# A recurrent mixer by seven products: order of loads, low parts a pair ahead, a later scaling of each head's output

## The chip, the cores and the metric

The kernel runs on one core of a Trainium2 chip. The metric is device time in microseconds of one execution; lower is better. The engines are TensorE (PE, with its weight loads PEld), VectorE (DVE), ScalarE (ACT), GpSimd (POOL) and SyncE (SP). Each works through its own queue in order; they meet by semaphores. DMA transfers are issued from the queues of SP and POOL here.

## The reference

One step of a two-layer decoder trunk on 512 prompt tokens and 8 x 4 new tokens, 544 columns in all, width 1024, all in f32. Layer 0 is a Mamba-2 mixer and a squared-ReLU MLP, layer 1 an HGRN2 mixer and another MLP, each behind an RMS norm and added to the residual. The change is in the HGRN2 mixer:

```python
proj = (u @ w_in).astype(jnp.float32)            # 1024 -> 4096: q, f, v, g
q = silu(proj[..., :F]); fz = proj[..., F:2*F]; v = proj[..., 2*F:3*F]; g = proj[..., 3*F:]
logf = logaddexp(log_sigmoid(fz), log(max(lb, 1e-20)) + log_sigmoid(-fz))
k = (1.0 - lb) * sigmoid(-fz)
o, s = hgrn_chunk_scan(q, k, v, logf, state)     # S_t = diag(f_t) S_{t-1} + k_t v_t^T ; o_t = S_t^T q_t
o = group_rmsnorm(o, norm_w, 8) * silu(g)        # 8 heads of 128
return o @ w_out, s
```

The states of the prompt and of the 8 sequences are outputs too.

## The kernel before, in words

Activations lie transposed: eight tiles `x[k]` of 128 features x 544 columns. f32 products are made of three products of a rounded format: both operands are split into a rounded high part and a rest, and high x high, high x low and low x high are added in PSUM. A unit of weights is a piece of 128 x 1024 (512 KB). There are three ways to a low part. `split` rounds the piece on ACT (`hi`) and subtracts on DVE (`lo = raw - hi`), in halves of 512 columns. Units in `by_load` have ACT write the negated rounded piece and a DMA from POOL add the weight to it in memory (L251, L252). Units loaded already rounded (kind "c", a DMA of POOL that converts, L205) do the same as one piece in `low_ahead` (L286, tile `lo`, one buffer).

The mixer's input has 32 units, four for each of 8 heads (q, f, v, g). The first four (head 0) are plain products (`product`, `project`). The other 28 are 14 pairs: two units with both halves of the rows and columns make a 2 x 2 block product that is done with seven products ("forms") instead of eight, in the order of `SLOTS`: p1, p2, n6, q7, n5, p3, q4, each 12 matmuls of 128 x 272, and pairs overlap: p1, p2 of pair i, then p3 of i-1, n6, q7 of i, q4 of i-1, n5 of i. p1 and p2 use the rounded piece ("c") and its `lo`; the other five use sums of pieces: `v` holds two halves of 512 columns, to which POOL DMAs add a third half (kind "va", L212); "a22" is a half by itself (L208); `s2 = v + a22` on DVE (tile `s`, L303), to which another POOL DMA adds later (L311). Each of the five is then split on ACT and DVE (`fh_*`, `fl_*`).

The list `loads` gives the order of loads and `jobs` that of conversions. A conversion calls loads up to three places past its own (`at + 3`), and `ahead` runs conversions until four halves wait for use. Instructions written out are then put in each engine's order by a planner that has its own costs and issues what is ready by them, so an instruction can run well ahead of its place in the text. Tiles of one tag share `bufs` buffers; a new one waits for the last use of the old. `mx` tiles are four PSUM banks (tag "mx"); `acc` tiles are two pairs of banks.

Between the matmuls, `tick()` runs background generators, two ticks per form. `operands` (norm, sums of halves) and `split_sums` prepare the right-hand sides. For each head `levels` computes the attention inside 128-token chunks by doubling (tiles `pa`, `K`, `q`, `T`), started by `complete` when f is there, with a wait in ticks, and `states` the rest: masks the values for eight sequences (`vm`), chunk states (`pS`, `S`), output (`po`, `pzs`), mean square (`oms`), its power -1/2 on POOL (`or`, L1626), scaling into `o2` (in the profile `o`, L1627 and L1630), then new states by two matmuls `pn` with four DVE updates `hst` each (L1637), and transposing back (`pt`). Last comes the output projection (`pho`), 8 units in two halves of heads. DVE's `f`, `g` and so on (L1441 to L1445) collect the seven products from PSUM and set its banks free.

Of the kernel before, what the change touches and what calls it, by code (L numbers as in the profile page):

```python
# [112 lines left out]
def trunk(ctx: ExitStack, tc: tile.TileContext, io):  # L113
# [58 lines left out]


    by_load = {ub + i for ub in (U_MLP, U_MLP2) for i in (1, 2, 3, 4, 5, 6, 8, 9)}
    by_load |= set(range(U_HGRN_IN, U_HGRN_IN + 4)) | set(range(U_HGRN_OUT, U_MLP2))
    plans = [plan_mlp(U_MLP, False)]
    hgrn_pairs, hgrn_forms = _hgrn_plan(U_HGRN_IN)
    pair_at = {u: i for i, u in enumerate(hgrn_pairs)}
    loads += [("u", U_HGRN_IN + i) for i in range(3)] + [("c", hgrn_pairs[0]), ("u", U_HGRN_IN + 3)]
    at = {x: len(loads) + i for i, x in enumerate(loads[-5:], -5)}  # L180
    for u in range(U_HGRN_IN, U_HGRN_IN + 4):
        jobs.append((("u", u), at["u", u]))
    for i, u in enumerate(hgrn_pairs):
        loads += [(kind, v) for kind, j in (("v", i), ("c", i + 1), ("va", i), ("a22", i)) for v in hgrn_pairs[j : j + 1]]
        at |= {x: len(loads) + i for i, x in enumerate(loads[-4:], -4)}
    for name, u in hgrn_forms:
        jobs.append(((name, u), at[{"p1": "c", "p2": "c", "q4": "a22", "n6": "a22"}.get(name, "va"), u]))
    for u in range(U_HGRN_OUT, U_MLP2):
        loads.append(("u", u))
        jobs.append((("u", u), len(loads) - 1))  # L190
# [95 lines left out]
    def low_ahead(u):  # L286

        hi = loaded["c", u]
        lo = mp["w"].tile([P, 1024], F32R, tag="lo12", bufs=1, name=f"lo{u}")
        nc.scalar.activation(lo, hi.bitcast(F32), AF.Copy, scale=-1.0)  # L290
        nc.gpsimd.dma_start(lo, io["W"][u], accum_op=ADD)
        lows[u] = lo

    def pair_form(name, u):

        i = pair_at[u]
        if name in ("p1", "p2"):
            c = slice(0, 512) if name == "p1" else slice(512, 1024)
            return [loaded["c", u][:, c]], [lows[u][:, c]]
        v = loaded["v", u]  # L300
        if name == "n6":
            s2 = mp["w"].tile([P, 512], F32, tag="s2", bufs=1, name=f"s2_{u}")
            nc.vector.tensor_tensor(s2, v[:, 512:], loaded["a22", u], ADD)  # L303
            loaded["s2", u] = s2
        raw = {"n6": ("s2", 0), "q7": ("v", 512), "n5": ("v", 0), "p3": ("s2", 0), "q4": ("a22", 0)}[name]
        raw = loaded[raw[0], u][:, raw[1] : raw[1] + 512]
        hi = wcv.tile([P, 512], F32R, tag="whi", name=f"fh{u}_{name}")
        lo = wcv.tile([P, 512], F32R, tag="wlo", name=f"fl{u}_{name}")
        split(raw, hi, lo)
        if name == "q7":  # L310
            nc.gpsimd.dma_start(loaded["s2", u], io["W"][u][:, 512:], accum_op=ADD)  # L311
        if name == "n5" and i + 1 < len(hgrn_pairs):
            low_ahead(hgrn_pairs[i + 1])
        return [hi], [lo]

    def form(name, u):
# [947 lines left out]
    def hgrn(then):  # L1264
# [91 lines left out]
        def product(u):  # L1356
            w = unit(u)
            ps = acc_tile(f"ps{u}")
            products(ps, w, uops, True, True, run=8, every=3)
            state["live"] -= 2  # L1360
            return ps

# [20 lines left out]
        def complete(u):  # L1383

            h, j = divmod(u - u0, 4)
            hc = slice(h, h + 1)
            d = heads[h]
            if j == 0:
                gate(d["q"], f"sq{h}")
            if j == 1:  # L1390
                f = d["f"]
                K = d["K"] = pool.tile([P, 640], F32, tag="K", bufs=2, name=f"K{h}")
                nf = K[:, :T]
                nc.scalar.activation(nf, f, AF.Sigmoid, scale=-1.0)
                nc.scalar.activation(f, f, AF.Sigmoid)
                nc.vector.scalar_tensor_tensor(f, nf, lbf[:, hc], f, MUL, ADD)
                nc.vector.tensor_tensor(d["QQ"][:, 1], d["q"], f, MUL)
                nc.scalar.activation(nf, nf, AF.Copy, scale=olb[:, hc])
                background(levels(h, d["QQ"], K, f, d), f"hl{h}", wait=2.5)
            if j == 2:  # L1400
                d["vz"] = d["v"]
            if j == 3:
                gate(d["g"], f"sg{h}")
# [8 lines left out]
        def seventh(name, u):  # L1412
# [6 lines left out]
                d["b"] = mx(f"hb{u}")[:, :HF]  # L1419
            ps = d[{"p2": "b", "q7": "c", "q4": "c"}.get(name, "a")]  # L1420
            hi, lo = take((name, u))
            n = 0
            for k in range(4):
                oh, ol = fops[name, k]
# [7 lines left out]
                        tick()  # L1432
            if name not in ("p1", "p2"):
                state["live"] -= 1
            keep = {"p1": "s1", "n6": "sv", "n5": "sw"}.get(name)
            with tc.high_priority():
                if keep:
                    d[keep] = pool.tile([P, HF], F32, tag=keep, bufs=1 + (keep == "sv"), name=f"{keep}_{u}")
                    nc.scalar.copy(d[keep], ps)
                if name == "p2":  # L1440
                    nc.vector.tensor_tensor(target(u)[:, :HF], ps, d["s1"], ADD)  # L1441
# [125 lines left out]
        def states(h, d):  # L1567
# [7 lines left out]
            for c in range(4):  # L1575
# [4 lines left out]
            o2 = pool.tile([P, 5, P], F32, tag="o2", name=f"o2{h}")  # L1580
            qm = o2[:, :2].rearrange("p a (b c) -> p (a b) c", c=NS)
            nc.vector.tensor_tensor(qm, Q[:, sc].unsqueeze(1).to_broadcast([P, SEQS, NS]), seqcol, MUL)
            vm = pool.tile([P, SEQS, P], F32R, tag="vm", name=f"vm{h}")
            nc.vector.tensor_tensor(
                vm, vq.unsqueeze(1).to_broadcast([P, SEQS, P]), seqrow.unsqueeze(2).to_broadcast([P, SEQS, P]), MUL
            )
            yield pace
            pS = mx(f"pS{h}")
            for c in range(4):
# [34 lines left out]
            nc.vector.tensor_scalar(ms, ms, 1.0 / P, EPS, MUL, ADD)  # L1624
            r = pool.tile([P, 5], F32, tag="or", bufs=2, name=f"or{h}")
            nc.gpsimd.tensor_tensor(r, ms, half, ALU.pow)  # L1626
            nc.vector.tensor_tensor(  # L1627
                o2[:, :4], po.rearrange("p (a b) -> p a b", b=P), r[:, :4].unsqueeze(2).to_broadcast([P, 4, P]), MUL
            )
            nc.vector.tensor_scalar(o2[:NS, 4], pzs[:NS, :P], r[:NS, 4:5], None, MUL)  # L1630
            yield pace
            for i in range(2):
                pn = mx(f"pn{h}_{i}")
                nc.tensor.matmul(pn, kq, vm[:, 4 * i : 4 * i + 4].rearrange("p s v -> p (s v)"), start=True, stop=True)
                for j in range(4):
                    s = 4 * i + j
                    nc.vector.scalar_tensor_tensor(st[:, s], st[:, s], Ts[:, s : s + 1], pn[:, j * P : (j + 1) * P], MUL, ADD)  # L1637
                yield pace
            nc.sync.dma_start(io["hgrn_s"][h], st)
            yield pace  # L1640
# [237 lines left out]
```

## Time and profile before

| | |
|---|---|
| median of 3 runs | 1531.43 us (1529.78 to 1533.83) |
| profiled execution | 1532.86 us, its span 1531.1 us |
| granted TensorE clock, mean over the span | 0.987 |
| busy: PE, DVE, ACT, POOL | 97%, 83%, 62%, 19% |
| second mixer | about 814 to 1156 us |
| its transfers | 59.35 MB, 173 GB/s |

In the profile a row of waits reads: engine, line, "<-" what it waited for, microseconds in total, how often, the longest. A row of a timeline: start, length, engine, line, operation, tiles written <- read, and in brackets the idle time before it and what ended it. A row of one line's instructions has durations in ns (least/median/most). Tile names are without numbers; several tiles can have one name (`hb` and `hp` are accumulators of the seven products, `ps` those of the plain ones).

### The profile page before, as it was taken

Reading aid. Unit: us, or ns where it says so; the run is one execution under the profiler, and the core shown is the slowest. Engines: PE = TensorE matmul, PEld = TensorE weight load, DVE = VectorE, ACT = ScalarE, POOL = GpSimd, SP = SyncE. Lnnn points to the kernel's source line nnn. Section 1 sums busy time; section 2 is a strip of 40 time slices with the busy share of each in tenths; the row PEclk is TensorE's granted clock in tenths of the full one; section 3 lists DMA queues with packets and bytes.
Section 4 is the critical chain, followed back from the end, with each engine's and each line's share of the span. In section 5 each row is a group of like instructions: output and inputs, shape, how many; then the busy total and the mean of one; then the engine's idle time right before and its main releaser. Section 6 shows DMA issues by size and latency. Waiting matters only on the chain. (4 is left out here: it accounts for less than half of the span.)

```text
span 1531.1 us, 33266 instructions
## 1 busy us (share of the span) xinstructions
PE 1482.8 (97%) x12956; PEld 1414.5 (92%) x12956; DVE 1276.8 (83%) x2486; ACT 946.9 (62%) x1928; POOL 290.1 (19%) x392
## 2 busy tenths in 40 slices
PE   8999899999999999999998899999999999999996
PEld 7898889898999999999997788888898999999996
DVE  7978899879777879898898778888856989888895
ACT  5685756757447657585776445455555758576673
POOL 3122012120012111111103123332222111111101
PEclk9999999999999999999999999999999999999998
DMA  6376557483557565675749477878568567575741
GB/s 193 94 198 169 163 129 207 128 223 105 153 154 153 128 179 145 173 179 139 191 113 234 102 180 174 188 179 206 128 157 202 125 172 179 138 186 137 184 115 66
DMA packets 106862, 243.77 MB, mean 159 GB/s; under 512 B 18064, under 2 KB 22064, under 8 KB 106704
## 3 DMA queue, kind: packets, MB, share of 16 engines
q1 hardware_dynamic: 66560, 158.17, 31.3%
q0 software_dynamic: 38880, 82.33, 30.5%
q8 instruction: 102, 1.67, 0.4%
q10 hardware_dynamic: 1264, 1.14, 0.2%
q14 instruction: 56, 0.46, 0.1%
HBM read 224.41 MB, written 17.18 MB: 158 GB/s over the span
## 5 line engine op out<-in xcount | busy, mean ns | idle before, releaser
L220 POOL DMA_DIRECT2D v<-in_W x94 | 82.2, 1018 | 468.1 <-DVE fl_p L232 130.9
L405 PE MATMUL ps<-uh_s,whi 128*128 128x272 f32 x576 | 124.4, 297 | 4.2 <-DVE BC L603 2.4
L405 PE MATMUL ps<-ul_s,whi 128*128 128x272 f32 x576 | 120.1, 289 | 0.0
L231 ACT CAST whi<-raw 128x512 fp32r<-128x512 f32 x114 | 70.0, 616 | 79.1 <-PE ps L405 40.6
L405 PEld LDWEIGHTS ps<-uh_s,whi 128*128 128x128 f32 x576 | 90.2, 188 | 11.8 <-issue 8.5
L256 ACT CAST whi<-raw 128x512 fp32r<-128x512 f32 x90 | 55.3, 617 | 70.2 <-PE ps L405 20.9
L232 DVE TENSOR_TENSOR wlo<-raw,whi 128x512 fp32r<-128x512 f32 x114 | 80.0, 704 | 22.1 <-ACT whi L231 20.5
L405 PEld LDWEIGHTS ps<-ul_s,whi 128*128 128x128 f32 x576 | 90.4, 188 | 0.6 <-issue 0.3
L232 DVE TENSOR_TENSOR fl_p<-raw,fh_p 128x512 fp32r<-128x512 f32 x94 | 64.1, 689 | 28.9 <-ACT fh_p L231 24.5
L405 PE MATMUL ps<-uh_s,wlo 128*128 128x272 f32 x576 | 85.2, 288 | 0.0
L231 ACT CAST fh_p<-raw 128x512 fp32r<-128x512 f32 x94 | 57.6, 619 | 37.8 <-PE pp L1176 20.8
L252 POOL DMA_DIRECT2D wlo<-in_W x56 | 49.1, 941 | 164.8 <-ACT wlo L251 153.6
L405 PEld LDWEIGHTS ps<-uh_s,wlo 128*128 128x128 f32 x576 | 77.3, 188 | 1.0 <-issue 0.8
L596 DVE SCALAR_TENSOR_TENSOR cacc<-pre,vh,cacc 128x568 f32<-128x568 f32 x72 | 57.8, 802 | 5.8 <-ACT cacc L594 5.3
L231 ACT CAST fh_n<-v 128x512 fp32r<-128x512 f32 x61 | 37.8, 619 | 37.2 <-PE pp L1176 32.9
L231 ACT CAST fh_p<-s 128x512 fp32r<-128x512 f32 x61 | 37.8, 620 | 34.8 <-PE pc_q L1176 27.3
L284 POOL DMA_DIRECT2D wlo<-in_W x34 | 30.1, 1044 | 146.9 <-ACT wlo L281 133.6
L405 PE MATMUL po<-yh,whi 128*128 128x272 f32 x256 | 55.7, 298 | 1.2 <-ACT yh L231 1.2
L232 DVE TENSOR_TENSOR fl_n<-s,fh_n 128x512 fp32r<-128x512 f32 x61 | 42.1, 690 | 16.0 <-ACT fh_n L231 11.7
L1176 PE MATMUL pp<-m_tl,fh_n 128*128 128x272 f32 x192 | 55.3, 288 | 0.0
L1176 PE MATMUL pc_q<-m_th,fh_q 128*128 128x272 f32 x192 | 55.3, 288 | 0.0
L1176 PE MATMUL pc_q<-m_th,fl_q 128*128 128x272 f32 x192 | 55.3, 288 | 0.0
(549 smaller groups left out, 5836.0 us busy)
## 6 DMA issues: line engine op xcount, KB each, us to landing
raw<-in_W SPq DMA_DIRECT2D x147, 512.0 KB, 4.5
v<-in_W SPq DMA_DIRECT2D x122, 256.0 KB, 4.5
v<-in_W POOLq DMA_DIRECT2D x122, 256.0 KB, 5.6
wlo<-in_W POOLq DMA_DIRECT2D x90, 256.0 KB, 6.1
a<-in_W SPq DMA_DIRECT2D x61, 256.0 KB, 4.6
w<-cum_d POOLq DMA_DIRECT2D x16, 512.0 KB, 7.7
st<-in_ssm_in SPq DMA_DIRECT2D x16, 512.0 KB, 4.6
out_ssm_s<-st SPq DMA_DIRECT2D x16, 512.0 KB, 6.1
```

Of the source, the lines that this page charges most:

```text
L220: nc.gpsimd.dma_start(raw[:, c : c + 512], io["W"][u + 1][:, :512], accum_op=ADD)
L231: nc.scalar.copy(hi, raw)
L232: (eng or nc.vector).tensor_tensor(lo, raw, hi.bitcast(F32), SUB)
L252: nc.gpsimd.dma_start(lo[a], io["W"][u][:, 512 * a : 512 * a + 512], accum_op=ADD)
L256: nc.scalar.copy(hi[a], c)
L284: nc.gpsimd.dma_start(lows[u][a], io["W"][u][:, 512 * a : 512 * a + 512], accum_op=ADD)
L405: nc.tensor.matmul(ps[:, h, :HF], block(a, c0 + k * step), o[:, h * HF : (h + 1) * HF], start=(first and i == 0), stop=(last and i == len( ...
L596: nc.vector.scalar_tensor_tensor(acc, pre[:, i : i + 568], vh[:, wc + 24 * i : wc + 24 * i + 1], acc, MUL, ADD)
L1176: nc.tensor.matmul(ps, block(w, k * P), o, start=(name_ in ("p1", "p2", "q7") and k == 0 and j == 0), stop=(k == 3 and j == 2), skip_group ...
```

## The change

- Of the mixer's four plain units only the third and fourth make their low part by load; the first two are split on DVE, and their products go piece by piece (high, low of each k) instead of all high parts first (`run`). Of the eight output units the last four are split too.
- The order of loads: all four plain units, then the first rounded piece; for each pair "a22" comes before "va", and the list for pair 0 is written apart. n6 now takes its place in the list from "va" instead of from "a22".
- `lo` has two buffers; the next pair's is asked for behind the matmuls of p1, instead of with the conversion of n5. `s1` and `sw` share one buffer.
- The wait ahead of `levels` is 4.5 ticks instead of 2.5.
- `vm` is made in two halves of four sequences. The mean square's scale and offset go to POOL. `o` is scaled behind the first four state updates, followed by the second half of `vm`.

```diff
-    by_load |= set(range(U_HGRN_IN, U_HGRN_IN + 4)) | set(range(U_HGRN_OUT, U_MLP2))
+    by_load |= {U_HGRN_IN + 2, U_HGRN_IN + 3} | set(range(U_HGRN_OUT, U_HGRN_OUT + 4))
...
-    loads += [("u", U_HGRN_IN + i) for i in range(3)] + [("c", hgrn_pairs[0]), ("u", U_HGRN_IN + 3)]
-    at = {x: len(loads) + i for i, x in enumerate(loads[-5:], -5)}
+    loads += [("u", U_HGRN_IN + i) for i in range(4)] + [("c", hgrn_pairs[0])]
+    loads += [(kind, hgrn_pairs[j]) for kind, j in (("v", 0), ("c", 1), ("a22", 0), ("va", 0))]
+    at = {x: len(loads) + i for i, x in enumerate(loads[-9:], -9)}
...
-    for i, u in enumerate(hgrn_pairs):
-        loads += [(kind, v) for kind, j in (("v", i), ("c", i + 1), ("va", i), ("a22", i)) for v in hgrn_pairs[j : j + 1]]
+    for i in range(1, len(hgrn_pairs)):
+        loads += [(kind, v) for kind, j in (("v", i), ("c", i + 1), ("a22", i), ("va", i)) for v in hgrn_pairs[j : j + 1]]
...
-        jobs.append(((name, u), at[{"p1": "c", "p2": "c", "q4": "a22", "n6": "a22"}.get(name, "va"), u]))
+        jobs.append(((name, u), at[{"p1": "c", "p2": "c", "q4": "a22"}.get(name, "va"), u]))
...
-        lo = mp["w"].tile([P, 1024], F32R, tag="lo12", bufs=1, name=f"lo{u}")
+        lo = mp["w"].tile([P, 1024], F32R, tag="lo12", bufs=2, name=f"lo{u}")
...
-        if name == "n5" and i + 1 < len(hgrn_pairs):
-            low_ahead(hgrn_pairs[i + 1])
...
-            products(ps, w, uops, True, True, run=8, every=3)
+            products(ps, w, uops, True, True, run=8 if u in by_load else 0, every=3)
...
-                background(levels(h, d["QQ"], K, f, d), f"hl{h}", wait=2.5)
+                background(levels(h, d["QQ"], K, f, d), f"hl{h}", wait=4.5)
...
+            if name == "p1" and u != hgrn_pairs[-1]:
+                low_ahead(hgrn_pairs[pair_at[u] + 1])
...
-                    d[keep] = pool.tile([P, HF], F32, tag=keep, bufs=1 + (keep == "sv"), name=f"{keep}_{u}")
+                    d[keep] = pool.tile([P, HF], F32, tag="sv" if keep == "sv" else "sw", bufs=1 + (keep == "sv"), name=f"{keep}_{u}")
...
-            vm = pool.tile([P, SEQS, P], F32R, tag="vm", name=f"vm{h}")
...
+            def values_of(i):
+                vm = pool.tile([P, 4, P], F32R, tag="vm", name=f"vm{h}_{i}")
...
+            vm = values_of(0)
...
-            nc.vector.tensor_scalar(ms, ms, 1.0 / P, EPS, MUL, ADD)
+            nc.gpsimd.tensor_scalar(ms, ms, 1.0 / P, EPS, MUL, ADD)
...
-            nc.vector.tensor_tensor(
-                o2[:, :4], po.rearrange("p (a b) -> p a b", b=P), r[:, :4].unsqueeze(2).to_broadcast([P, 4, P]), MUL
-            )
-            nc.vector.tensor_scalar(o2[:NS, 4], pzs[:NS, :P], r[:NS, 4:5], None, MUL)
             yield pace
             for i in range(2):
...
+                if i == 0:
+                    nc.vector.tensor_tensor(
+                        o2[:, :4], po.rearrange("p (a b) -> p a b", b=P), r[:, :4].unsqueeze(2).to_broadcast([P, 4, P]), MUL
+                    )
+                    nc.vector.tensor_scalar(o2[:NS, 4], pzs[:NS, :P], r[:NS, 4:5], None, MUL)
+                    vm = values_of(1)
                 yield pace
```

More of the change, by code (lines that the diff above doesn't have):

```diff
@@ L294, in pair_form @@
     def pair_form(name, u):
-        i = pair_at[u]
         if name in ("p1", "p2"):
-            c = slice(0, 512) if name == "p1" else slice(512, 1024)
-            return [loaded["c", u][:, c]], [lows[u][:, c]]
+            return None, None
         v = loaded["v", u]
@@ L1421, in seventh @@
             hi, lo = take((name, u))
+            if name in ("p1", "p2"):
+                c = slice(0, 512) if name == "p1" else slice(512, 1024)
+                hi, lo = [loaded["c", u][:, c]], [lows[u][:, c]]
             n = 0
@@ L1582, in states @@
             nc.vector.tensor_tensor(qm, Q[:, sc].unsqueeze(1).to_broadcast([P, SEQS, NS]), seqcol, MUL)
-            vm = pool.tile([P, SEQS, P], F32R, tag="vm", name=f"vm{h}")
-            nc.vector.tensor_tensor(
-                vm, vq.unsqueeze(1).to_broadcast([P, SEQS, P]), seqrow.unsqueeze(2).to_broadcast([P, SEQS, P]), MUL
-            )
+            def values_of(i):
+                vm = pool.tile([P, 4, P], F32R, tag="vm", name=f"vm{h}_{i}")
+                nc.vector.tensor_tensor(
+                    vm, vq.unsqueeze(1).to_broadcast([P, 4, P]),
+                    seqrow[:, 4 * i : 4 * i + 4].unsqueeze(2).to_broadcast([P, 4, P]), MUL,
+                )
+                return vm
+            vm = values_of(0)
             yield pace
@@ L1623, in states @@
             nc.scalar.activation(o2[:NS, 4], pzs[:NS, :P], AF.Square, accum_out=ms[:NS, 4:5])
-            nc.vector.tensor_scalar(ms, ms, 1.0 / P, EPS, MUL, ADD)
+            nc.gpsimd.tensor_scalar(ms, ms, 1.0 / P, EPS, MUL, ADD)
             r = pool.tile([P, 5], F32, tag="or", bufs=2, name=f"or{h}")
             nc.gpsimd.tensor_tensor(r, ms, half, ALU.pow)
-            nc.vector.tensor_tensor(
-                o2[:, :4], po.rearrange("p (a b) -> p a b", b=P), r[:, :4].unsqueeze(2).to_broadcast([P, 4, P]), MUL
-            )
-            nc.vector.tensor_scalar(o2[:NS, 4], pzs[:NS, :P], r[:NS, 4:5], None, MUL)
             yield pace
@@ L1633, in states @@
                 pn = mx(f"pn{h}_{i}")
-                nc.tensor.matmul(pn, kq, vm[:, 4 * i : 4 * i + 4].rearrange("p s v -> p (s v)"), start=True, stop=True)
+                nc.tensor.matmul(pn, kq, vm.rearrange("p s v -> p (s v)"), start=True, stop=True)
                 for j in range(4):
@@ L1637, in states @@
                     nc.vector.scalar_tensor_tensor(st[:, s], st[:, s], Ts[:, s : s + 1], pn[:, j * P : (j + 1) * P], MUL, ADD)
+                if i == 0:
+                    nc.vector.tensor_tensor(
+                        o2[:, :4], po.rearrange("p (a b) -> p a b", b=P), r[:, :4].unsqueeze(2).to_broadcast([P, 4, P]), MUL
+                    )
+                    nc.vector.tensor_scalar(o2[:NS, 4], pzs[:NS, :P], r[:NS, 4:5], None, MUL)
+                    vm = values_of(1)
                 yield pace
```

## The prediction

> **What bounds the kernel now.** I read the page first, then the stretches of the changed stage, what TensorE (PE) waited for in it, the chain that ended last, and the engines' queues in order of time.
>
> ```profile
> span 1531.1 us, 33266 instructions
> PE 1482.8 (97%) x12956; PEld 1414.5 (92%) x12956; DVE 1276.8 (83%) x2486; ACT 946.9 (62%) x1928; POOL 290.1 (19%) x392
> ```
>
> PE is busy nearly all of the span, so only time in which PE stands still, or runs at a low clock, can be won. The second mixer lasts from 814 to 1156 us. Its stretches (PE, PEld, DVE, ACT, POOL busy; granted clock; DMA share; GB/s):
>
> ```profile
> 813.00:850.00 37.00, 31.51 (x325) 29.56 (x324) 32.27 (x79) 21.24 (x40) 13.31 (x20) 0.95 0.86 206
> 850.00:892.00 42.00, 33.33 (x302) 30.09 (x301) 28.84 (x70) 21.08 (x51) 10.11 (x13) 0.88 0.61 124
> ...
> 992.00:1026.00 34.00, 33.27 (x419) 30.11 (x420) 28.97 (x77) 18.54 (x47) 11.56 (x15) 1.00 0.80 190
> ```
>
> The first 79 us hold the loss: 14.2 us without PE and a lowered clock. A head in the steady part loses 0.7 us of 34. PE's waits in the whole stage:
>
> ```profile
> PE hp L1426 <- DMA lo<-in_W: 4.2, 1, 4.2
> PE ps L405 <- DVE q L1407: 3.9, 1, 3.9
> PE hp L1426 <- DVE f L1445: 2.9, 1, 2.9
> PE pn L1634 <- DVE o L1627: 2.7, 4, 1.2
> PE hp L1426 <- DVE hn_tl L232: 1.5, 2, 0.8
> PE ps L405 <- DMA wlo<-in_W: 1.4, 1, 1.4
> PE pa L1487 <- ACT K L1398: 1.2, 2, 0.6
> PE pa L1487 <- DVE K L1518: 0.7, 2, 0.5
> ```
>
> They sum to 18.5 us. Three of them are followed by a slow clock:
>
> ```profile
> 834.00:837.00 3.00, 2.66 (x12) 2.69 (x13) 3.00 (x6) 2.72 (x5) 0.74 (x1) 0.50 1.13 207
> ...
> 863.00:868.00 5.00, 4.80 (x21) 4.80 (x22) 0.15 (x1) 0.00 (x0) 0.00 (x0) 0.51 0.40 67
> ...
> 888.00:892.00 4.00, 3.53 (x16) 3.53 (x17) 3.96 (x11) 3.24 (x6) 0.92 (x1) 0.57 0.38 41
> ```
>
> From the chain, start and length, the links around the second and third of these, and a form (12 matmuls) at full clock:
>
> ```profile
> 855.59 0.96 ACT lo L290
> ...
> 856.84 6.31 DMA lo<-in_W
> ...
> 875.68 6.86 DMA v<-in_W
> ...
> 884.82 1.26 POOL or L1626
> ...
> 888.07 0.36 DVE f L1445
> ...
> 902.46 1.50 PE hp L1426 x12
> ```
>
> A matmul costs 1.50 / 12 = 0.125 us. So the 21, 16 and 12 matmuls of the slow stretches would need 2.6, 2.0 and 1.5 us instead of 4.8, 3.5 and 2.7: the clock costs 2.2, 1.5 and 1.2 us. Waits and clock together, 23.4 us, are all that this stage can give back while PE's work stays.
>
> **The change part by part.** These rows carry the terms: waits of other engines, then prices, then queue positions.
>
> ```profile
> POOL v L212 <- DMA v<-in_W: 28.3, 6, 8.3
> ACT lo L290 <- PE hb L1426: 24.0, 12, 3.5
> DVE o L1627 <- POOL or L1626: 14.4, 8, 4.7
> ...
> DVE x L512 <- PE pho L405: 8.7, 6, 2.3
> ```
>
> ```profile
> L290 ACT ACTIVATE lo<-raw x14: 1057/1060/1067, 821.8 to 1063.6; 128x1024 fp32r<-128x1024 f32 x14
> L232 DVE TENSOR_TENSOR wlo<-raw,whi x2: 681/683/685, 1150.9 to 1151.5; 128x512 fp32r<-128x512 f32 x2
> L1637 DVE SCALAR_TENSOR_TENSOR hst<-hst,T,pn x64: 325/329/346, 887.0 to 1123.0; 128x128 f32<-128x128 f32 x64
> L1624 DVE TENSOR_SCALAR oms<-oms x8: 159/160/174, 881.3 to 1119.3; 128x5 f32<-128x5 f32 x8
> L1584 DVE TENSOR_TENSOR vm<-vq,h_seqrow x8: 1214/1218/1220, 873.8 to 1103.1; 128x1024 fp32r<-128x1024 f32 x8
> ```
>
> ```profile
> L231 ACT CAST fh_p<-raw 128x512 fp32r<-128x512 f32 x94 | 57.6, 619 | 37.8 <-PE pp L1176 20.8
> ```
>
> ```profile
> v<-in_W POOLq DMA_DIRECT2D x28, 256.0 KB, 5.7
> ...
> lo<-in_W POOLq DMA_DIRECT2D x14, 512.0 KB, 7.8
> ```
>
> ```profile
> 825.05 1.48 DVE L1326 SCALAR_TENSOR_TENSOR hn_n<-x,vec,hn_rb 128x544 f32<-128x544 f32 x2 [2.24 <-ACT hn_rb L470]
> ...
> 833.47 0.72 DVE L1407 TENSOR_TENSOR q<-ps,hn_rb 128x544 f32<-128x544 f32 x1
> ...
> 1007.86 1.75 POOL L212 DMA_DIRECT2D v<-in_W  x2 [7.04 <-DVE g L1381]
> ...
> 1017.97 0.69 DVE L303 TENSOR_TENSOR s<-v,a 128x512 f32<-128x512 f32 x1
> ...
> 1026.78 0.69 DVE L1627 TENSOR_TENSOR o<-po,or 128x512 f32<-128x512 f32 x1 [1.32 <-POOL or L1626]
> ```
>
> (a) Second buffer for `lo`, asked for behind p1 of the pair before. Today the single buffer is free only when p2 has ended, so ACT stands for 24.0 us over 12 pairs and the second pair's DMA, begun at 856.8, lands at 863.15, when PE has stood 4.2 us. With two buffers the negated copy (1.06 us) needs only the loaded piece and can go some forms earlier; 1.06 + 7.8 us then lie beside one period of a pair. Late next is DVE: `hn_tl` already holds PE for 1.5 us just before. Bounds: 0 (DVE late by as much) to 4.2 + 2.2 = 6.4. The DVE was idle in 863 to 868 (0.15 us busy), so it was not behind by more than what it had just finished; I take 5.5. In the steady part PE waits for no `lo`, so that gain is nothing there.
>
> (b) `o` scaled behind four states, mean of squares on POOL. Four state updates at 0.33 (about 1.1 us pipelined) go into DVE's wait for `or`, 14.4 us over 8 heads. PE feels that wait twice: 2.9 + 1.5 us at 885 to 892, where `or` was late behind transfers of `v`, `o` behind `or`, and `f`, which frees PE's accumulator, behind `o`; and 2.7 us at `pn`. Halving `vm` adds one fixed cost, 2 x 0.69 (the 128x512 row of `s`) - 1.22 = 0.16 us per head on DVE. The second half stands behind `o`, so the second `pn` needs `o` and 0.69 more. Moving 0.16 us from DVE to POOL makes `or` later, by between 0.16 and the 1.26 of `or`; take 0.3. Bounds: gain 4.4 + 2.7 = 7.1; loss 8 x (0.69 + 0.16) = 6.8, if each head's second `pn` waits for its values. I take 3.0 from 885 to 892, and 0.5 from `pn`.
>
> (c) `levels` two ticks (one form, 1.5 us) later, heads 1 to 7 only, because for head 0 the queue is not empty. The waits of `pa` for K, 1.2 + 0.7, should go; bounds 0 to 1.9, take 1.0. Head 7 ends some 1.5 us later, hidden by the first half of the output products (DVE waits there for PE, 8.7 us).
>
> (d) The first two units split on DVE, by the plain order of products. Four negated copies and four POOL DMAs (1 MB) go; DVE gets 4 x 0.68 = 2.7 us. The 1.4 us for `wlo` goes but is worth nothing: right behind it PE waits for `q` at 833.47, the end of a DVE sequence that began at 825.05. The extra splits fall before that; DVE idles 2.24 us there. Bounds: -0.5 (ACT free sooner) to +2.7; take +0.3.
>
> (e) Loads. The fourth whole unit comes before the first rounded piece: one POOL and one SP issue swap, and ACT's first `lo` waits for a piece that starts later; in (d)'s bound. `a22` is asked for a pair earlier on SP and waits there for its buffer; behind it on SP stand `v` and the states' loads. `va` stands one place later on POOL. In the rows, the pair's two `v` additions were issued at 1007.86 and the sum `s` ran at 1017.97, so 10.1 us lie between for an issue of 1.75 and a landing of 5.7: 2.7 us of slack. I take 0: the tile planner places an issue when its data are there, whatever its place in the text, and this one needs only `v`.
>
> (f) Units 4 to 7 of the output by splits: 8 x 0.68 = 5.5 us for DVE, hidden in the 8.7 us that it waits for PE, 0. The shared buffer of `s1` and `sw` makes the copy of `s1` wait for a subtraction one form earlier, 0. ACT gets 24 us back, but PE waits for ACT only in (c).
>
> Sum: -5.5 - 3.5 - 1.0 + 0.3 = -9.7 us. The profiled execution took 1532.86 us (span and 1.8 around it), 1.4 above the median of 1531.43. So the profiled form would be 1523.2, the median 1521.7; I say 1522.
>
> By the Trainium skill, page "TensorE: Matmul & The Clock Gate", section "What's actually happening", the clock falls to half after an idle window of about 3.4 us and comes back after as long a busy one. The trace disagrees on the threshold: 2.9 us before 888 were enough for 0.57. By that rule the 1.5 us would not belong to that wait, and my sum would be about 1 us smaller, 1523.
>
> **The rivals.**
> Covered: the start stays bound by DVE, `hn_tl` takes the place of `lo`, and `or` stays behind `v` on POOL. For it: DVE is busy 32.3 of the first 37 us, and gets 2.7 more. Against it: the idle DVE at 863. Only about 1.5 of (a), 0.5 of (b) and (c) are left: -2, 1529.5.
>
> Late `va`, slower: POOL really issues the additions at their new place, in front of n6 of the same pair. n6 comes five forms later, 7.5 us; the sum (0.69), a cast (0.62) and a split (0.68) take 2 of it, 5.5 are left, and 1.75 + 5.7 = 7.5 are needed. It decides once the slack of 2.7 us is used up. With 2 us late at 13 pairs, 26 us in part hidden, say 16 shown: 1521.7 + 16 = 1538. Against it: 28.3 us of POOL waiting for `v` show that the issues stand ready far ahead.
>
> Banks, slower: `po` and `pzs` are held behind four more DVE updates, and the four small PSUM banks also serve `pn`, `hb` and `pa`. At +1.1 to 1.5 us a head on PE, 8 heads give +10: 1532 to 1534, thus no change to slightly slower. For it: PE waits for `o` at `pn` already, which is a bank set free.
>
> **How the numbers follow.** Chances: forecast 0.62 (1513 to 1526), covered 0.17, late `va` 0.10, banks 0.11, of which 0.05 slower. A measurement here tells about 0.3%, 4.6 us, from no change. Faster 0.64, same 0.21, slower 0.15. The range: all of (a) to (c) and the 1.5 us of `hn_tl` gone gives 1531.4 - 6.4 - 7.1 - 1.9 - 1.5 = 1514.5, with (d)'s 0.5 and a little more 1513; the top takes in covered and half of the banks, 1533.
>
> **What would show it.** Right: no PE wait for `lo`, a clock of 1.00 in 855 to 870, ACT no longer waiting for `hb`, the wait of `o` for `or` well under 14.4 us, and the stage of 342 us about 10 shorter. Wrong: DVE waiting for DMA `v` ahead of `s` (late `va`); PE waiting for `vm` or for DVE at `pa` and `hb` (banks); a later first `hn_n` on DVE (the start lost more than 0.3). It would be wrong altogether if the planner's new order shifted the steady heads, where PE has 0.7 us of 34 to spare and all that is added there is paid eight times.

## The result and the profile after

The changed kernel takes 1540.13 us (median of 19 runs) against 1531.43 us for the kernel before, run beside it: ratio 1.005, 95% interval 1.0033 to 1.0066, so 0.5% slower. The forecast was 1522, with 1533 as the top of its range. The profiled execution took 1540.4 us.

```profile
span 1538.6 us, 33263 instructions
...
PE 1485.0 (97%) x12956; PEld 1416.6 (92%) x12956; DVE 1282.3 (83%) x2498; ACT 942.2 (61%) x1916; POOL 279.7 (18%) x388
```

The matmuls are the same. Of the 7.5 us that the span is longer, 2.2 are longer busy time of PE with them, at a mean clock of 0.984 for 0.987; the rest is standing still. The stretches of the mixer in the changed kernel (busy time of PE, PEld, DVE, ACT, POOL; granted clock; DMA share; GB/s):

```profile
813.00:850.00 37.00, 25.45 (x170) 24.17 (x169) 27.65 (x64) 19.75 (x36) 10.39 (x13) 0.77 0.83 203
850.00:892.00 42.00, 37.26 (x448) 33.65 (x447) 32.85 (x82) 20.98 (x50) 10.59 (x15) 1.00 0.59 121
992.00:1026.00 34.00, 33.21 (x420) 29.83 (x419) 28.85 (x77) 18.92 (x47) 11.17 (x15) 1.00 0.81 191
```

The first 37 us have 6.1 us less PE work than before, at a clock of 0.77 for 0.95; the next 42 have 3.9 more, at 1.00 for 0.88. The windows are not quite alike: the stage (its first `hn_pc` matmul) began at 823.0 us in this execution and at 818.7 in the one before. Of these 4.3 us, 1.2 lie ahead of the first matmul of the MLP before the stage (463.2 for 462.0) and 3.1 in that MLP. Counted from its own start, the stage loses 5.3 us up to the first p1, wins 5.0 from there to the third pair's p1 and loses 4.5 in the steady heads. So the gain that was forecast around the second pair is there, and a loss stands on each side of it. The 3.1 us in the MLP are there in the fastest kernel below too (f6: 360.2 us from the MLP's first matmul to the stage, here 359.8, before 356.7), so they are not what the experiments win back, and their cause was not looked for.

What engines waited for, in the order in which it is used below:

```profile
PE ps L402 <- DVE q L1404: 10.9, 1, 10.9
...
DVE s L302 <- DMA v<-in_W: 6.1, 1, 6.1
...
ACT lo L291 <- DMA raw<-in_W: 5.6, 2, 3.9
...
PE hp L1426 <- ACT sv L1441: 7.4, 6, 3.1
...
ACT fh_p L232 <- DMA s<-in_W: 8.7, 5, 3.5
...
PE pn L1639 <- DVE vm L1589: 4.3, 2, 4.0
...
DVE o L1644 <- POOL or L1635: 19.9, 8, 6.1
...
ACT lo L291 <- PE hb L1426: 21.1, 11, 4.1
```

PE no longer waits for `lo` (4.2 before), but for `q` 10.9 instead of 3.9, for `sv` 7.4 and for `vm` 4.3, both new. Three places in the engines' queues account for these.

**The first 20 us.** DVE's queue:

```profile
826.82 0.30 DVE L431 SCALAR_TENSOR_TENSOR hn_rb<-hn_rb 128x136 f32<-128x136 f32 x1
833.22 0.69 DVE L302 TENSOR_TENSOR s<-v,a 128x512 f32<-128x512 f32 x1 [6.09 <-DMA v<-in_W]
833.83 1.48 DVE L1323 SCALAR_TENSOR_TENSOR hn_n<-x,vec,hn_rb 128x544 f32<-128x544 f32 x2
```

The sum `s` of the first pair, first read 14 us later, stands ahead of the first `hn_n` and waits for an addition on its way; behind it stand all operands and `q`. In the kernel before it stood behind them. ACT has the same fault: `lo` stands ahead of the copy that `hn_n` needs. It did so in the kernel before too, where it waited 2.68 us for its piece.

```profile
826.51 1.06 ACT L291 ACTIVATE lo<-raw 128x1024 fp32r<-128x1024 f32 x1 [3.89 <-DMA raw<-in_W]
...
828.51 0.65 ACT L467 COPY hn_rb<-hn_pr 128x272 f32<-128x272 f32 x2
```

And on SP the fourth unit's load stands ahead of `v` until DVE's splits set a buffer free (7.6 us), so the first pair's loads start at 816.62:

```profile
808.16 0.38 SPq L1272 DMA_DIRECT2D bmask<-in_bmask  x1
816.24 0.33 SPq L202 DMA_DIRECT2D raw<-in_W  x1
816.62 0.42 SPq L217 DMA_DIRECT2D v<-in_W  x1
```

**The states.** Head 0, on DVE, then POOL, then PE:

```profile
889.66 0.69 DVE L1644 TENSOR_TENSOR o<-po,or 128x512 f32<-128x512 f32 x1 [6.05 <-POOL or L1635]
890.26 1.11 DVE L1642 SCALAR_TENSOR_TENSOR hst<-hst,T,pn 128x128 f32<-128x128 f32 x4
...
891.90 0.67 DVE L1589 TENSOR_TENSOR vm<-vq,h_seqrow 128x512 fp32r<-128x512 f32 x1
```

```profile
886.34 1.75 POOL L213 DMA_DIRECT2D v<-in_W  x2 [8.05 <-DMA v<-in_W]
887.50 0.83 POOL L1633 TENSOR_SCALAR oms<-oms 128x5 f32<-128x5 f32 x1
888.42 1.21 POOL L1635 TENSOR_TENSOR or<-oms,h_half 128x5 f32<-128x5 f32 x1
```

```profile
892.63 0.50 PE L1639 MATMUL pn<-vm,kq 128*128 128x512 f32 x1 [3.95 <-DVE vm L1589]
```

In the text `o` is behind the first four states. In DVE's queue it is ahead of them, here and in heads 1 to 6; only in head 7 does it follow them. POOL stands 8.05 us for a load in front of `oms`, so `or` is late, `o` waits, and states and the second half of `vm` wait behind `o`. So in seven heads of eight the main edit of part (b) was not carried out, and its side effect (second half of `vm` behind `o`) was.

**The steady heads.** ACT, and PE behind it:

```profile
1057.97 0.62 ACT L232 CAST fh_p<-s 128x512 fp32r<-128x512 f32 x1 [3.54 <-DMA s<-in_W]
1058.49 0.38 ACT L1441 COPY sv<-hp 128x272 f32<-128x272 f32 x1
```

```profile
1058.93 0.40 PE L1426 MATMUL hp<-hn_th,fh_q 128*128 128x272 f32 x1 [3.12 <-ACT sv L1441]
```

`fh_p`, needed later, stands ahead of the copy `sv` that frees PE's accumulator, and waits for the addition to `s`.

### The profile page after: what moved, and what is told of

Same layout as the page of the kernel before. It is cut to its first block, busy times and chain, and to the rows that moved or that the text cites. A ratio compares the mean times of both kernels' runs of the same rounds, so it can differ in the third digit from the quotient of the medians.

```text
span 1538.6 us, 33263 instructions
## 1 busy us (share of the span) xinstructions
PE 1485.0 (97%) x12956; PEld 1416.6 (92%) x12956; DVE 1282.3 (83%) x2498; ACT 942.2 (61%) x1916; POOL 279.7 (18%) x388
## 3 DMA queue, kind: packets, MB, share of 16 engines
q1 hardware_dynamic: 66560, 158.17, 31.7%
## 5 line engine op out<-in xcount | busy, mean ns | idle before, releaser
L233 DVE TENSOR_TENSOR wlo<-raw,whi 128x512 fp32r<-128x512 f32 x126 | 88.2, 703 | 24.9 <-ACT whi L232 23.4
L253 POOL DMA_DIRECT2D wlo<-in_W x44 | 39.6, 964 | 154.5 <-ACT wlo L252 136.2
L285 POOL DMA_DIRECT2D wlo<-in_W x34 | 30.1, 1043 | 148.6 <-ACT wlo L282 135.0
L1173 PE MATMUL pc_q<-m_tl,fh_q 128*128 128x272 f32 x192 | 55.2, 287 | 0.0
```

Of the source, the lines that this page charges most:

```text
L233: (eng or nc.vector).tensor_tensor(lo, raw, hi.bitcast(F32), SUB)
L253: nc.gpsimd.dma_start(lo[a], io["W"][u][:, 512 * a : 512 * a + 512], accum_op=ADD)
L285: nc.gpsimd.dma_start(lows[u][a], io["W"][u][:, 512 * a : 512 * a + 512], accum_op=ADD)
L1173: nc.tensor.matmul(ps, block(w, k * P), o, start=(name_ in ("p1", "p2", "q7") and k == 0 and j == 0), stop=(k == 3 and j == 2), skip_group ...
```

## The experiments

The kernel has a helper `pinned` that holds an instruction behind everything written before it on its engine; otherwise the planner is free. Every experiment that "holds" something uses it, and the arithmetic is the same in all. The fifth column has the median and the difference of medians to the kernel before, run beside each; the last has the interval of the ratio. The two can differ by up to 3 us (e4: 23.9 by the medians, 1.4% or 21 by the ratio), so a step of less than that between two kernels is doubtful. The columns between are from one profiled execution each, and those of e3 and e6 took 7.8 and 5.4 us more than their medians, that of e4 4.3 less. They go from the first `hn_pc` matmul to the first p1, from there to the third pair's p1, and from there to the last pair's. The stage began between 816.8 and 823.0 us in these executions, so places are counted from its own start, and what lies ahead of it is in none of these columns.

| kernel | to first p1 | to third | to last | median, difference | ratio to before, 95% |
|---|---|---|---|---|---|
| before | 31.1 | 38.7 | 185.4 | | |
| changed | 36.4 | 33.7 | 189.9 | 1540.1, +8.7 | 1.0033 to 1.0066 |
| e1 s held | 39.1 | 33.4 | 191.8 | 1541.6, +9.3 | 1.0027 to 1.0061 |
| e2 (d) undone | 38.3 | 34.0 | 188.5 | 1540.2, +8.0 | 1.0024 to 1.0056 |
| e3 (d) undone, o ahead | 37.7 | 33.2 | 197.3 | 1540.2, +7.9 | 1.0027 to 1.0066 |
| e4 (a), vm in halves | 40.2 | 33.6 | 198.8 | 1556.2, +23.9 | 1.0116 to 1.0158 |
| e5 s, lo held | 29.9 | 38.7 | 190.9 | 1534.1, +2.8 | 1.0006 to 1.0033 |
| e6 e5, loads swapped back | 30.0 | 37.4 | 192.6 | 1535.4, +4.1 | 1.0010 to 1.0048 |
| e7 e5, fourth unit behind v | 29.5 | 36.8 | 190.5 | 1533.0, +1.7 | 0.9997 to 1.0029 |
| e8 e6, (d) undone | 31.7 | 35.7 | 188.8 | 1535.0, +3.7 | 1.0004 to 1.0030 |
| e9 e7, o ahead | 30.7 | 34.1 | 193.2 | 1532.9, +0.5 | 0.9987 to 1.0021 |
| e10 e7, o held behind | 29.4 | 32.0 | 184.8 | 1522.8, -9.6 | 0.9906 to 0.9949 |
| e11 e7, lo asked earlier | 29.4 | 38.3 | 188.9 | 1535.7, +3.3 | 1.0000 to 1.0028 |
| e13 e10, additions held | 30.6 | 32.7 | 235.4 | 1569.7, +37.3 | 1.0216 to 1.0265 |
| f1 changed, o held behind | 36.8 | 29.5 | 189.5 | 1532.5, +0.1 | 0.9993 to 1.0016 |
| g1 before, o held behind | 31.1 | 36.8 | 183.8 | 1529.2, -3.2 | 0.9970 to 0.9998 |
| f3 e10, (a) and holding undone | 30.8 | 34.3 | 194.4 | 1532.1, -0.4 | 0.9989 to 1.0015 |
| f4 e10, (c) undone | 29.6 | 31.5 | 190.6 | 1526.9, -5.5 | 0.9954 to 0.9983 |
| f5 e10, (d) undone | 32.1 | 32.3 | 184.4 | 1525.2, -7.5 | 0.9936 to 0.9968 |
| f6 e10, changed order of loads | 30.5 | 31.8 | 183.2 | 1522.8, -9.9 | 0.9921 to 0.9960 |

### One cause at a time (e1 to e4)

e1, the changed kernel with

```diff
-            nc.vector.tensor_tensor(s2, v[:, 512:], loaded["a22", u], ADD)
+            ins = nc.vector.tensor_tensor(s2, v[:, 512:], loaded["a22", u], ADD)
+            if u == hgrn_pairs[0]:
+                pinned(ins)
```

> The changed kernel with one line altered: the sum s of the first pair may not be placed ahead of what stands before it in the text on VectorE, so it stands behind the first two projections instead of ahead of the first hn_n. Theory H (the loss at the start is that one place in VectorE's queue, 6.1 us of standing there, of which about 2.2 would go to the wait for the copy of hn_rb in any case): the first hn_n about 4 us earlier, PE's wait for q down from 10.9 to about 6, the start of the first p1 about 4 us earlier and 3 to 5 us off the time of the changed kernel, 1535 to 1537. Rival X (VectorE's extra splits and the rounded piece that comes behind the fourth whole unit make the start late, s only fills the hole): the time stays within 1 us of 1540.

Measured: nothing won. DVE's hole is gone, but ACT is the next in line; its queue in e1:

```profile
823.95 1.06 ACT L291 ACTIVATE lo<-raw 128x1024 fp32r<-128x1024 f32 x1 [5.94 <-DMA raw<-in_W]
...
825.96 0.65 ACT L469 COPY hn_rb<-hn_pr 128x272 f32<-128x272 f32 x2
...
835.22 1.06 ACT L291 ACTIVATE lo<-raw 128x1024 fp32r<-128x1024 f32 x1 [6.42 <-DMA raw<-in_W]
```

The copies of the first and of the second pair stand ahead of `hn_rb` and of the second `hn_b1h`; the second one has a buffer to go to only since `lo` has two. DVE waits for the copies behind them, 4.12 and 5.75 us, and PE 13.1 us for `q`. X had the time right, for another reason.

e2, part (d) undone in the changed kernel:

```diff
-    by_load |= {U_HGRN_IN + 2, U_HGRN_IN + 3} | ...
+    by_load |= set(range(U_HGRN_IN, U_HGRN_IN + 4)) | ...
```

> The changed kernel with part (d) alone undone for the first stage: all four first units get their low parts by the negated copy and the adding DMA again. Theory H: s falls back behind the first hn_n by itself, the hole of 6.1 us goes, and VectorE's splits leave the tail of the first MLP; the HGRN stage starts about 2 us earlier and the first p1 6 to 9 us earlier than in the changed kernel: 1531 to 1534. Rival X expects 3 us or less from it, 1537 or more, with PE still waiting about 8 us for q because the rounded piece comes behind the fourth unit. Theory S (the steady heads lose 4.5 us to part (b)) holds in both: the distance between the p1 of the third and of the last pair stays at 189.9 us, where the kernel before had 185.4.

Measured: within 1 us of the changed kernel. `s` falls back behind `hn_n`, as H said, and ACT stands instead: the first `lo` waits 7.49 us for its piece, until 831.25, and PE 12.3 us for `q`. H was right on the order and wrong on the price.

e3, e2 with `o` ahead of the states in the text and `oms` on DVE:

> The run before it with the order of the states undone as well: o is scaled ahead of the first four states again and the mean of squares is on VectorE again; vm stays in two halves, the second made behind the first four states. Theory S (part (b) costs the steady heads: or comes later by way of POOL, 19.9 us of waiting for it against 14.4, and the second half of vm stands behind o, 4.3 us of PE): 3 to 5 us less than the run without the splits, PE's wait for vm gone, the distance from the third pair's p1 to the last pair's down from 189.9 to 186 us, about 1528. Rival T (the steady loss is from the later additions va and from ACT, which keeps PE waiting 7.4 us for the copy sv): no change within 1 us, and the waits for sv stay at 7 us.

Measured: the same as e2. S failed: PE still waits 4.3 us for `vm`, and DVE's wait of `o` fell from 19.9 to 13.6 us without moving the time, so its length alone is no measure of the loss. T's waits for `sv` stayed, and grew to 11.0 us in this execution. That part (b), as the planner lays it out, is worth nothing in either direction fits its not being carried out.

e4, of the whole change only the two buffers of `lo`, their place behind p1, the buffer shared by `s1` and `sw`, and `vm` in halves:

> The second buffer of lo and its earlier place alone, with what it needs for room (shared buffer of s1 and sw, vm in halves): the order of loads, the splits, the wait of the levels, the place of o and of the mean of squares are those of the kernel before. Term (a) put this at -5.5 us, between 0 and -6.4: PE's wait of 4.2 us for lo and the half clock behind it go. Theory A (the gain is real and the other parts took it): 1525 to 1528, no PE wait for lo, granted clock 1.00 in the 15 us behind the first pair. Rival C (the start is bound by VectorE, hn_tl takes the place of lo): 1530 or more, with PE waiting some 3 us for hn_tl in that place.

Measured: 23.9 us slower than the kernel before, outside both theories. PE waits no more for `lo`, and pays elsewhere: 12.5 us for `q`, 7.2 in 6 waits for `vm`, and mostly in the steady heads

```profile
ACT fh_p L231 <- DMA s<-in_W: 16.2, 6, 4.9
...
DVE fl_p L232 <- ACT fh_p L231: 12.1, 5, 4.3
...
PE hp L1425 <- ACT sv L1440: 10.0, 4, 4.7
```

Term (a) left to the planner, with the halves of `vm` that make room for it, is the costliest part of the change; the other parts give back two thirds of it. What (a) costs without the halves was not run.

### Holding what waits for transfers (e5 to e8)

e5, the changed kernel with `s` of the first pair held as in e1, and

```diff
-        nc.scalar.activation(lo, hi.bitcast(F32), AF.Copy, scale=-1.0)
+        pinned(nc.scalar.activation(lo, hi.bitcast(F32), AF.Copy, scale=-1.0))
```

> The changed kernel with two things held in text order: the first pair's s on VectorE (as in the first experiment) and every negated copy lo on ScalarE, so that lo is neither placed ahead of the copies of hn_rb and hn_b1h nor, in the steady heads, right behind hb of the pair before. Theory Q (in-order queues: lo and s stand ahead of work that is ready, waiting for transfers): ScalarE's waits of lo for raw (5.6 us, 12.4 in the first experiment) and for hb (21.1) go, PE's wait for q falls from 11 to 13 us to 7 or less, the first p1 comes 4 to 6 us earlier, and 4 to 7 us come off the changed kernel: 1533 to 1536. Rival L (the loads are late whatever waits for them, because the fourth whole unit's load stands ahead of v on SP's queue): the first p1 within 2 us of the first experiment's, 1538 to 1541.

Measured: 6 us off the changed kernel, the first p1 6.5 us sooner after the stage's start, PE's wait for `q` 4.7. Q holds for the wait and the time, though PE now waits 4.0 us for the second pair's `lo`, whose held place is too late: from the first to the third p1 it takes 38.7 us again, where the changed kernel took 33.7. So by these two executions the stage as a whole is only 0.5 us shorter (259.5 for 260.0); where the 6 us of the medians lie they do not show.

e6 and e7, e5 with other orders of loads (lines cut and names shortened):

```diff
 e6
-    ... for i in range(4)] + [("c", hgrn_pairs[0])]
+    ... for i in range(3)] + [("c", hgrn_pairs[0]), ("u", U_HGRN_IN + 3)]
 e7
+    loads += [("u", U_HGRN_IN + i) for i in range(3)] + [("c", hgrn_pairs[0])]
+    loads += [("v", p0), ("a22", p0), ("u", U_HGRN_IN + 3), ("c", p1), ("va", p0)]      # p0, p1: first pairs
```

> The kernel of the run before it, and the first rounded piece is loaded ahead of the fourth whole unit again (that one swap in the list of loads undone; VectorE still splits the first two units). Rival L, now beside Q: SP no longer stands 7.6 us for the buffer of the fourth unit ahead of v, the first v is issued at about 808 instead of 816, the first rounded piece some 5 us earlier, and the start wins 3 to 5 us more than the pins alone: 1529 to 1533. If Q alone is the cause, within 1 us of the run before.

> The pins, and the fourth whole unit is asked for behind the first pair's v and a22, so that on SP nothing of the first pair stands behind its buffer. Theory L expects as much as from the swap or 1 to 2 us more (a22 comes ahead of the second half of v): 1528 to 1532. Theory Q alone expects nothing beside the pins. If the fourth unit itself becomes late, PE waits for its low part (wlo or whi) for 2 us or more, which neither run before shows.

Measured: +1.3 and -1.1 us against e5, inside what the runs can tell. SP's 7.6 us cost nothing once nothing stands waiting for these loads in front of ready work: L fell.

e8, e6 with (d) undone:

> The pins, the swap of the loads undone, and part (d) undone as well for the first stage: VectorE splits neither of the first two units. If VectorE's two extra splits in the tail of the first MLP cost what they seem to (stage begins 2 us later in the changed kernel), 1 to 3 us less than the run with pins and swap: 1527 to 1531. If they are hidden, the same within 1 us; if ScalarE and the queue of POOL were the tighter ones, 1 to 3 us more, since four negated copies and four transfers of 256 KB come back ahead of the first pair's.

Measured: the same as e6 within 0.4 us.

With the copies held the steady heads stay at 190 us: PE's wait for `sv` falls from 7.4 to 0.5 us (e7), and another wait comes out. It is not the order of `fh_p` and `sv` that changed: `sv` stands right behind a `fh_p` at 12 of 14 pairs, at 13 in the changed kernel. But ACT now waits only 0.4 us there for the addition to `s`, instead of 8.7. That addition lands sooner (a median of 4.1 us from issue to landing in e7, 6.4 in the changed kernel); why was not traced. Waits of e7:

```profile
DVE o L1646 <- POOL or L1637: 21.3, 8, 5.9
...
PE hb L1428 <- DVE o L1646: 8.0, 5, 2.0
...
PE pn L1641 <- DVE vm L1591: 4.3, 2, 3.8
```

### The order of o (e9 to e13)

e9, e7 with `o` ahead of the states in the text and `oms` on DVE; e10, e7 with (lines shortened)

```diff
                 if i == 0:
-                    nc.vector.tensor_tensor(o2[:, :4], po..., MUL)
-                    nc.vector.tensor_scalar(o2[:NS, 4], pzs..., MUL)
-                    vm = values_of(1)
+                    vm = values_of(1)
+                    pinned(nc.vector.tensor_tensor(o2[:, :4], po..., MUL))
+                    pinned(nc.vector.tensor_scalar(o2[:NS, 4], pzs..., MUL))
```

> The kernel with the pins and the fourth unit behind v and a22 (1532.95 us), and part (b) undone: o is scaled ahead of the states and the mean of squares is on VectorE; vm stays in halves. Theory B (banks: o keeps po's PSUM bank until or has come, and PE, which waits 8.0 us in 5 heads for hb's bank, pays for it): the wait of hb for o falls to 2 us or less, 5 to 8 us come off, 1526 to 1528. Rival Z (o stands ahead of the states on VectorE in the changed kernel already, as its queue shows in 7 of 8 heads, so nothing moves): within 1.5 us of 1533, hb still waiting for o some 7 to 8 us.

> The kernel with the pins and the fourth unit behind, and part (b) carried out for good: the second half of vm is asked for ahead of o, and both scalings of o are held behind it, so that on VectorE the order is four states, second half of vm, o. Theory V (PE's 4.3 us for vm are the half that stands behind o behind or): that wait goes, 3 to 4 us off the start of the steady heads. Theory B (banks) expects hb's wait for o to grow from 8.0 by 1 to 2 us a head, thus 10 to 16 us: together 1534 to 1540. If the banks don't matter, 1528 to 1530.

Measured: e9 is within 1.2 us of e7, as Z said. e10 is 10 us faster than e7 and 9.6 faster than the kernel before. V was right on the wait, and its 3 to 4 us are a third of what came; B was wrong: PE's waits for `vm` and for `hb` are both gone. Head 0 in e10, DVE and POOL:

```profile
878.21 1.12 DVE L1644 SCALAR_TENSOR_TENSOR hst<-hst,T,pn 128x128 f32<-128x128 f32 x4 [2.28 <-PE pn L1641]
879.25 0.68 DVE L1591 TENSOR_TENSOR vm<-vq,h_seqrow 128x512 fp32r<-128x512 f32 x1
...
881.93 0.69 DVE L1647 TENSOR_TENSOR o<-po,or 128x512 f32<-128x512 f32 x1 [1.64 <-POOL or L1637]
```

```profile
878.63 1.73 POOL L213 DMA_DIRECT2D v<-in_W  x2 [8.24 <-DMA v<-in_W]
879.83 0.78 POOL L1635 TENSOR_SCALAR oms<-oms 128x5 f32<-128x5 f32 x1
```

`or` is as late as ever behind `v` on POOL. What changed is that DVE has other work in front of it: its wait of `o` over all heads is 1.6 us instead of 21.3.

e11, e7 with the second pair's `low_ahead` called behind `operands` instead of behind the first p1:

> The kernel with the pins and the fourth unit behind, and the second pair's lo asked for earlier: behind the operands hn instead of behind the first p1. Theory A (the second pair's lo lands 3.3 us late because its place behind p1 is too late there; the gain of term (a) is real once the copy is neither too early nor too late): PE's wait of 3.3 us for lo goes, with 1 to 2 us of half clock behind it, 1528 to 1530. Rival: hn_tl takes its place (VectorE), 1 us or less is won.

Measured: no gain, and no test. Earlier in the text came out later on ACT (32.4 us after the stage's start, against 29.5 in e7), with ready casts put ahead of it; PE waited 4.3 us for `lo`.

e13, e10 with the two additions `va` of each pair held in text order on POOL:

> The run with o held behind, and the additions va held in text order on POOL: for the first head the mean of squares and or then stand ahead of the third pair's additions instead of behind them, where they waited 8 us for v. Theory P (or is late because POOL stands in order for a transfer): VectorE's longest wait of o for or, 5.9 us, goes to 2 us or less, and 2 to 4 us come off against the run before it. Rival: the additions come later for every pair, so s and fh_p are late, ScalarE waits for s more than 8 us, and the time is 3 us or more above the run before it.

Measured: 47 us slower than e10. It is the rival's direction, far above the 3 us that it named:

```profile
POOL s L312 <- DVE fl_n L233: 134.0, 14, 14.2
ACT fh_n L232 <- DVE s L302: 53.7, 11, 8.2
```

Holding helps only where the text's order is a good one. Here it put the additions, from the third pair on, behind the addition to `s` of the pair before; in e10 they stand ahead of it.

### Term by term (f1 to f6)

> The changed kernel with nothing altered but the order on VectorE in the states: four states, second half of vm, then o, held there. Theory O (VectorE's 19.9 us of standing in front of o for or is what the steady heads lose): the wait goes below 4 us, PE's 4.3 us for vm goes, third to last p1 falls from 189.9 to 184 to 186 us, and 5 to 10 us come off: 1530 to 1535. The start keeps its loss: PE's wait for q stays at 10 to 13 us. Rival C (ScalarE's copies of lo are what holds the steady heads): 1537 or more, with PE still waiting 7 us for sv.

f1 (e10's edit alone in the changed kernel): 7.6 us faster than the changed kernel, level with the kernel before. In its execution 4.2 us of the gain came between the first and the third pair; the steady heads stay at 189.5 us with 8.3 us of PE waiting for `sv`, and PE's wait for `q` is 11.3. So O has about half, C the rest: with only the copies held the steady heads wait for `hb`, with only `o` held for `sv`, and only with both do they fall to 185.

> The kernel before with one part of the change alone, and held: o is scaled behind the first four states (vm whole, mean of squares on VectorE as before). Term (b) put this at -3.5 us, of which 0.16 us a head for halving vm is not paid here: 1526 to 1529, VectorE's wait of 14.4 us of o for or down to 3 or less, PE's 2.7 us at pn and 2.9 us for f gone. Banks, the rival: PE waits for hb or pn by 1 us a head, 1532 or more.

g1 (the kernel before, `o` held behind the first four states, nothing else): 3.2 us faster, by its interval 0.3 to 4.6. DVE's wait of `o` falls from 14.4 to 3.8. No bank wait appears.

> The best kernel so far (o held, pins, fourth unit behind, 1522.8 us) with term (a) undone: one buffer for lo, asked for with n5 of the pair before, its copy free to stand as early as the planner likes. Term (a) at its forecast size: 4 to 6 us more, 1526 to 1529, PE waiting 4 us or more for the second pair's lo and ScalarE 20 us or more for hb. Rival (with o held, VectorE or the transfers are the bound and the second buffer is worth nothing): within 1.5 us of 1523.

f3 (e10 with `bufs=1` for `lo`, asked for with n5, copies after the first free): 9.3 us slower than e10. `lo` costs PE 5.4 us (3.0 in e10), `sv` 6.0 (2.9), and the steady heads take 194.4. This undoes two things, the second buffer and, but for the first copy, the holding; the holding of `s` and the copies alone moves about 10 us (f1 to f6). So f3 does not show what the second buffer is worth: one buffer with held copies was not run.

> The best kernel so far with term (c) undone: the levels begin two ticks sooner again (2.5 for 4.5). Term (c) at its size: 1 us more, 1523 to 1525, PE waiting 1 to 2 us for K at pa. If the wait is worth nothing: within 0.5 us; if the levels' delay costs at the end of the last head, 1 us less.

f4 (e10 with `wait=2.5`): 4.1 us slower, four times the forecast for (c). PE waits for K at `pa` only 1.9 us of it; the steady heads take 5.8 us longer, so most of the price comes by way of the queues being laid out anew. By which link was not traced.

> The best kernel so far (pins, o held, fourth unit behind, 1522.8 us) with part (d) undone in the first stage: the first two units get their low parts by negated copy and adding DMA, as in the kernel before. Term (d) at its forecast size, +0.3 for the change: within 1 us of 1522.8. If VectorE's splits in the tail of the MLP are what makes the stage begin late: 1 to 3 us less. If the four negated copies and four transfers of 256 KB are the dearer form: 2 us or more above, with PE waiting about 1.4 us for wlo again.

f5 (e10, (d) undone): 2.1 to 2.4 us slower, near what can be told apart, and PE waits 1.2 us for `wlo` again, as the third case expected; (d) is a small gain if anything, not a loss.

> The changed kernel with its own order of loads (fourth whole unit ahead of the first rounded piece and of v), the copies s and lo pinned and o held: the best kernel so far without its altered loads. Term (e) as the prediction had it, 0: within 1.5 us of 1522.8. If the fourth unit's load, which keeps SP standing 7.6 us ahead of v, costs by itself: 2 to 4 us more, 1525 to 1527. The comparison of the two kernels with pins and without o held gave 1.1 us.

f6 (e10 with the changed kernel's own order of loads): the same as e10, 1522.84 us, ratio 0.994 to the kernel before. It differs from the changed kernel only in the held `s`, `lo` and `o`, with the second half of `vm` ahead of `o`. PE's waits of the stage in f6:

```profile
PE ps L404 <- DVE q L1406: 4.7, 1, 4.7
PE hp L1428 <- DMA lo<-in_W: 2.9, 1, 2.9
PE hp L1428 <- ACT sv L1443: 1.7, 2, 1.3
PE hp L1428 <- DVE g L1447: 1.7, 1, 1.7
```

The changed kernel, e5, f1 and f6 have one order of loads and make a square. By their differences to the kernel before, holding `s` and the copies wins 5.9 us, holding `o` 8.6, and both 18.6, about 4 more than the two apart.

## Why the prediction was wrong

The sum of -9.7 us is what the change gives when its order is the order in the queues (f6, -9.9; e10, -9.6). The changed kernel as written is 18.6 us away from that. The step that failed stands in (e), and (a) and (b) rest on it: "the tile planner places an issue when its data are there, whatever its place in the text". The planner places an instruction where its own costs say the data would be there. The engine then waits in order: `lo` 3.9 us ahead of `hn_rb`, `s` 6.1 ahead of `hn_n`, `o` 19.9 ahead of the states. Holding these three is worth 18.6 us. The prediction used the step to price moves at nothing; it should have been the reason to price them as unknown.

- **(a)**, -5.5: the gain is there (PE does not wait for `lo`; first to third p1 33.7 us for 38.7). Missed was what a second buffer allows: "the negated copy needs only the loaded piece and can go some forms earlier" is just what the planner used, too early at the start, ahead of `hn_rb`. "ACT no longer waiting for `hb`" failed too: 21.1 us for 24.0, because the copy moves on to the next time a buffer comes free, right behind `hb` again. Left to the planner, with `vm` in halves, it costs 23.9 us; held, its undoing together with the holding costs 9.3. The 5.5 by itself stays unmeasured.
- **(b)**, -3.5: that four state updates "go into DVE's wait for `or`" was not what the queue did in 7 heads of 8; the wait grew from 14.4 to 19.9 us. With the order held, g1 gives -3.2, near the term's size, but its interval goes from -0.3 to -4.6, and it halves no `vm`. The bound for the second `pn` ("needs `o` and 0.69 more") was right and came true once, 3.95 us. The scale on POOL took 0.20 us in seven heads and 0.83 in head 0, for 0.16 on DVE, so the 0.3 was ample but for head 0.
- **(c)**, -1.0: too small, 4.1 in the held kernel (f4), outside its own bound of 1.9, which counted only PE's waits for K.
- **(d)**, +0.3, and **(e)**, 0, are right within what runs can tell, but only in the held kernel. In the changed kernel as written (d) has a side effect that its working left out: with DVE's splits the planner puts `s` ahead of `hn_n`, and undoing (d) alone (e2) puts it back. The sign that was named, "a later first `hn_n` on DVE", showed: 10.8 us after the stage's start instead of 6.3.
- **Rivals.** "Late `va`" gave its sign, DVE waiting for DMA `v` ahead of `s`, yet once and not at 13 pairs, by `s` being early and not by `va` being late; its 1538 is near the result by chance. "Banks" showed with the copies held (8.0 us for `hb`) and went when `o` was held: the bank waited for `or`, not for four more updates. The last sentence, that the planner's new order might shift the steady heads, described the outcome and had no price.

That the sum agrees with f6 is no proof of each term: undone one by one in the held kernel, (a) with its holding, (b), (c) and (d) cost 9.3, about 10 (e9 to e10), 4.1 and 2.4, far more than 9.9 together, so the agreement is in part luck. Each kernel is laid out anew, and the losses are not independent. In the square above, undoing one of the holdings costs 10.0 or 12.7 us and undoing both 18.6, less than the two in sum: there one loss partly hides the other. Through which waits was not traced. How the start splits between DVE's and ACT's places in the changed kernel stays open: removing DVE's alone (e1, and e2 with (d) undone) moved nothing, and removing ACT's alone was not tried.

## What to carry to other kernels

Where a planner orders the queues, an edit to the text is a request: before pricing it, look where an instruction that waits for a transfer will stand in its engine's queue, and what ready work is behind it. More buffers and earlier requests can widen that risk, since they let a waiting instruction float further forward. Hold such instructions behind the work that must not wait, one line each, and judge the change by that kernel; the same holding in a poor order (e13) costs more than it can win.

## What the runs showed of the hardware

PE's clock does not fall by the length of a wait alone. Here are windows of the changed kernel behind the wait of 3.95 us that ended at 892.63 and behind the one of 3.12 us that ended at 1058.93 (granted clock third from the end), and the wait of the kernel before ahead of the stretch from 888 to 892, which had 0.57:

```profile
892.40:894.40 2.00, 1.77 (x9) 1.73 (x10) 2.00 (x5) 1.92 (x5) 0.93 (x1) 0.75 0.04 8
894.40:896.40 2.00, 2.00 (x10) 2.00 (x10) 2.00 (x6) 0.98 (x2) 0.03 (x1) 0.50 0.67 72
...
1058.60:1060.60 2.00, 1.67 (x13) 1.67 (x14) 1.38 (x2) 0.76 (x2) 0.00 (x0) 1.00 0.90 288
1060.60:1062.60 2.00, 2.00 (x19) 2.00 (x19) 1.33 (x3) 1.43 (x3) 0.00 (x0) 1.00 0.34 126
```

```profile
888.47 0.60 PE L1426 MATMUL hp<-hn_b1h,raw 128*128 128x272 f32 x1 [2.95 <-DVE f L1445]
```

The wait of 3.12 us cost no clock, while the one of 2.95 us in the kernel before halved it, and so did the one of 3.95. The Trainium skill, page "TensorE: Matmul & The Clock Gate", section "What's actually happening", says that the window of about 3.4 us is free-running. The trace fits that, if which waits cost depends on where they lie in the window, but no run here shows where it lay. A threshold on the wait's length, as the prediction weighed it, is not what these three waits show.

A scale and offset of 128x5 took 0.20 us on POOL in seven heads of the changed kernel, little more than the 0.16 on DVE before. In head 0, directly behind the issue of two DMAs, it took 0.83.
